# Requesting the later modulation weights from ScalarE's queue in a two-layer transformer step

## The chip, the cores and the metric

The kernel runs on one core of a Trainium2 chip, in one launch. The metric is the device time in microseconds. Three timed runs of the kernel before took 2960.68, 2961.05 and 2964.94 us. Beside them stands one profiled execution, from which all rows of the trace come.

A core has five engines that run side by side, each with its own stream of instructions in a fixed order: TensorE (PE, with its weight loads as PEld), VectorE (DVE), ScalarE (ACT), GpSimd (POOL) and SyncE (SP), which computes nothing and here requests transfers. A transfer between main memory and the core's own memory is requested by an instruction in the stream of one engine. If that instruction has to wait, everything behind it in the stream waits too. The data move later, on 16 DMA engines, and a semaphore tells when they have landed.

## The reference

One step of a diffusion backbone: two layers (DEPTH = 2) on 1024 sample tokens and 128 prompt tokens, width 1024, all in fp32. Cut to what matters here:

```python
def _modulation(cvec, w, b):
    m = (jax.nn.silu(cvec) @ w + b)[:, None, :]
    return jnp.split(m, 6, axis=-1)

def _layer(x, mod, lw, ctx):
    sh1, sc1, g1, sh2, sc2, g2 = mod
    h = _rms(x, n1) * (1 + sc1) + sh1
    u_conv, qa, ka, va, qn, kn, vn = jnp.split(h @ w_in, idx, axis=-1)
    ...
    x = x + g1 * (jnp.concatenate([a_out, b_out, c_out], axis=-1) @ w_out)
    h = _rms(x, n2) * (1 + sc2) + sh2
    x = x + g2 * (jnp.square(jax.nn.relu(h @ w1)) @ w2)
```

For each layer the modulation multiplies two conditioning vectors (one for the sample, one for the prompt) with a 1024 x 6144 matrix ada_w. The kernel cuts these 6144 columns into three groups of 2048: group 0 holds sh1 and sc1, which are needed at the start of the layer, group 1 holds g1 and sh2, group 2 sc2 and g2, which are needed after the attention.

## The kernel before

The program is written out in order by hand (the scheduler keeps the order of the source on every engine), with Python generators that are stepped in between one another. Waits and the choice of buffers are put in by the framework: a tile of the pool T gets one of 18 buffers of 128 x 512 fp32, and an instruction that writes a new tile waits until the last user of the buffer is done.

All transfers go through the helper `load` (L143), which takes an engine and uses SP where none is given. So SP requests everything: weights, stores of projections, loads for the attention, results.

`modulation(l, groups, first)` is a generator. Its `fetch` takes the next pair of group r and slab k of 128 rows of ada_w. In its later form (not `first`) it makes four T tiles `aw` of 128 x 512 and loads them (L203), 256 KB each. The generator fetches one slab ahead: a step runs the four matmuls of slab k (L224, shown as eight, since each fp32 matmul is two rows) into the bank `psmod`, and then fetches slab k + 1. After eight slabs a group is copied out and transposed. The first group of layer 0 goes another way (`first`, L198) and is not touched.

There are 40 fetches in three places. For layer 0, groups 1 and 2 (16 fetches) are stepped as `fill` from `project`; for layer 1, group 0 (8 fetches) is stepped from the last groups of layer 0's `mlp`, once for every two products, and groups 1 and 2 (16 fetches) again from `project`.

`project` multiplies the normed tokens with w_in, column block by column block: A0 to A5 and VN, each in five token groups of which the last is half as long. A token group on PE is `tok_group` (L548 to L550, rows `pst`). Behind it comes `post`: ACT squares (`sq`), DVE sums (`ss`), ACT takes logarithm and exponential (`y`), DVE refines and multiplies (`xn`), and POOL applies the gains and, in A0 and A1, the rotary embedding (L491 to L497, rows `o` and `t`). Between these stand steps of a convolution (rows `cacc`, `cp`). After the first, third and fifth group of a block `fill` is stepped once, and after every group `flush` requests the stores of `o` to `ddA` and `dvA` that are three groups old. After the second and fourth group's matmuls `pr.step` splits a piece of w_in (CAST `wh` on ACT, `wl` on DVE) and requests the next (`wr`). In A5 the first loads for the attention follow: keys `kd` and `cd`, values `v`, queries `qd`; the keys are transposed on PE (`pstr`, L791).

In `mlp` a product is 24 matmuls into a pair of banks (L1326), and `taken` moves it out, on ACT and DVE, to `ev`; `w1h` and `w1l` are the split weights of the products to come.

Of the kernel before, what the change touches and what calls it, by code (L numbers as in the profile page):

```python
# [45 lines left out]
def hybrid_step(ctx, tc, I, O, depth=DEPTH):  # L46
    nc = tc.nc
# [13 lines left out]
    def T(shape, dt=F32, n="t"):  # L61
        return pers.tile([128] + list(shape), dt, tag="T", bufs=N_T, name=nm(n))
# [24 lines left out]
    def P(n="ps"):  # L87
        return psum.tile([128, 512], F32, tag="p", bufs=8, name=nm(n))
# [9 lines left out]
    def tt(out, a, b, op, eng=None):  # L98
        (eng or nc.vector).tensor_tensor(out=out, in0=a, in1=b, op=op)  # L99

    def stt(out, a, s, b, op0, op1):
        nc.vector.scalar_tensor_tensor(out=out, in0=a, scalar=s, in1=b, op0=op0, op1=op1)  # L102
# [25 lines left out]
    def ada_b(l):  # L128
        return vecs[l][:, 0:48]

    def n1g(l):
        return vecs[l][:, 48:56]

    def n2g(l):
        return vecs[l][:, 56:64]
# [7 lines left out]
    def load(out, in_, eng=None):  # L143
        (eng or nc.sync).dma_start(out=out, in_=in_)
# [38 lines left out]
    def modulation(l, groups, first=False):  # L183

        todo = [(r, k) for r in groups for k in range(KT)]
        ready = []

        def fetch():
            if todo:
                r, k = todo.pop(0)  # L190
                if first:
                    if k % 2 == 0:
                        o = {0: 0, 2: 12, 4: 4, 6: 8}[k]
                        ready.extend([[HF[o + 2 * a + b][:, c:c + 512] for b in range(2) for c in (0, 512)] for a in range(2)])
                    o = {0: 0, 2: 12, 4: 4, 6: 8}[k - k % 2] + 2 * (k % 2)
                    for b in range(2):
                        c = r * 2048 + b * 1024
                        load(HF[o + b][:, 0:1024], I["ada_w"][l, k * 128:(k + 1) * 128, c:c + 1024])  # L198
                    return
                four = []  # L200
                for c in range(r * 2048, (r + 1) * 2048, 512):
                    aw = T([512], n="aw")
                    load(aw, I["ada_w"][l, k * 128:(k + 1) * 128, c:c + 512])  # L203
                    four.append(aw)
                ready.append(four)

        for _ in range(6 if first else 1):
            fetch()
        if first:
            ps = P("psmod")  # L210
            nc.vector.memset(ps, 0.0)
            yield
            fetch()
            fetch()
        yield
        for r in groups:
            if not first:
                ps = P("psmod")
                nc.vector.memset(ps, 0.0)
                yield  # L220
            for k in range(KT):
                aw = ready.pop(0)
                for j in range(4):
                    mm(ps[32 * j:32 * j + 2, :], silc[:, k, :], aw[j], start=(k == 0), stop=(k == KT - 1))  # L224
                if not first:
                    fetch()
                yield
            mt = T([512], n="mt")
            nc.vector.tensor_copy(mt, ps)
            yield  # L230
            pt = P("psmt")
            for b in range(4):
                nc.tensor.transpose(pt[:, b * 128:(b + 1) * 128], mt[:, b * 128:(b + 1) * 128], ident)
            ptv = pt.rearrange("p (b j x) -> p j b x", b=4, j=4, x=32)
            for s in range(2):
                tt(mod[l][:, s, r * 16:(r + 1) * 16].rearrange("p (j b) -> p j b", j=4), ptv[:, :, :, s],
                   ada_b(l)[:, r * 16:(r + 1) * 16].rearrange("p (j b) -> p j b", j=4), ALU.add)
            if r == 0:
                for s in range(2):
                    stt(A1[l][:, s, :], mod[l][:, s, 8:16], 1.0, n1g(l), ALU.add, ALU.mult)  # L240
            if r == 2:
                for s in range(2):
                    stt(A2[l][:, s, :], mod[l][:, s, 32:40], 1.0, n2g(l), ALU.add, ALU.mult)
            yield
# [1745 lines left out]
```

## Time and profile before

| | us |
|---|---|
| median of three timed runs | 2961.05 |
| lowest, highest | 2960.68, 2964.94 |
| the profiled execution | 2955.55 |
| its span, first to last instruction | 2953.8 |

The rows that the prediction quotes are of these kinds. The page gives busy times and the chain of work that ended last. The view of a tile gives, for all instructions that touch it, their number and their duration (least, median, most, in ns), the waits that it ended and, for transfers, the time from the request to the landing. A row of windows gives one stretch: its length, the busy time of PE, PEld, DVE, ACT and POOL with the number of instructions in brackets, PE's granted clock, the mean busy share of the DMA engines and GB/s. A row of the waits reads: who waited, for whom, us in total, how often, the longest. A row of the timeline reads: start, length, engine, line, operation, tiles written and read, shapes, how many instructions were merged, and in brackets the idle time of the engine before it and what ended it. SPq marks requests of SP; where several are merged into one row, its length contains the waits between them.

### The profile page before, as it was taken

The page shows a single profiled execution, that of the slowest core. Times are in us where ns is not written, and L with a number is a line of the kernel's source. Part 1 is how long each engine was busy: PE and PEld are TensorE (multiplying, and loading weights), DVE is VectorE, ACT ScalarE, POOL GpSimd, SP SyncE. Part 2 cuts the span into 40 slices and gives each one's busy share as a digit, 9 for nine tenths or more (in the row PEclk, how much of TensorE's full clock was granted, in tenths as well). Part 3 has the DMA queues.
Part 4 walks back from the last instruction along what each step waited for, and adds up shares of the span by engine and source line. Part 5 has one row for each costly group of instructions (what it writes and reads, how often), then busy time and mean ns, then how long its engine had stood idle before and what let it go on. Part 6 is the DMA issues. An engine that isn't in the chain of part 4 may idle for free.

```text
span 2953.8 us, 52917 instructions
## 1 busy us (share of the span) xinstructions
PE 2840.5 (96%) x20328; PEld 2520.6 (85%) x20328; DVE 2036.7 (69%) x4009; ACT 1413.2 (48%) x2924; POOL 658.6 (22%) x607
## 2 busy tenths in 40 slices
PE   6999999999999999999889999999999999999999
PEld 3879645899999989999878885458999999999999
DVE  6576778854867756668675757778467776585776
ACT  4335366762744443433452453668446444443343
POOL 3587346410000000000225772563100000000000
PEclk7999999999999999999989999999999999999999
DMA  7277202424466678542433781024345675665334
GB/s 289 81 217 195 83 22 56 103 83 134 159 204 220 193 241 302 164 149 91 139 123 105 191 219 50 17 69 99 97 122 196 199 221 176 217 226 183 114 105 161
DMA packets 434876, 444.05 MB, mean 150 GB/s; under 512 B 120512, under 2 KB 308672, under 8 KB 434624
## 3 DMA queue, kind: packets, MB, share of 16 engines
q1 hardware_dynamic: 434624, 440.67, 47.9%
q8 instruction: 160, 2.62, 0.4%
q14 instruction: 92, 0.75, 0.1%
HBM read 307.41 MB, written 133.17 MB: 149 GB/s over the span
## 4 chain that ended last, share of the span: by engine, by line
PE 82%; DVE 9%; ACT 3%; DMA 2%; issue 2%; POOL 2%; SPq 0%; DVEq 0%; POOLq 0%; ACTq 0%
PE ps L1326 24%; PE psb L1326 7%; PE psc L1326 6%; PE pso L1326 5%; PE psa L1326 5%; PE pst L548 4%; PE pst L549 3%; PE pst L550 3%; PE psd L1326 3%; PE psacc L1125 3%; PE pspv L992 2%; PE pspt L976 2%; PE psst L1139 2%; PE psmod L224 2%; PE psm L1051 2%
## 5 line engine op out<-in xcount | busy, mean ns | idle before, releaser
L1326 PE MATMUL ps<-ts,w2h 128*128 128x288 f32 x3072 | 535.5, 296 | 8.3 <-DVE ts L99 4.8
L1326 PEld LDWEIGHTS ps<-ts,w2h 128*128 128x128 f32 x3072 | 452.7, 189 | 9.3 <-DVE ts L99 5.3
L1326 PE MATMUL ps<-ts,w2l 128*128 128x288 f32 x1536 | 329.7, 296 | 0.0
L96 ACT CAST ts<-ti 128x576 fp32r<-128x576 f32 x256 | 172.1, 672 | 311.5 <-PE ps L1326 210.2
L548 PE MATMUL pst<-wh,HA 128*128 128x256 f32 x1040 | 295.4, 284 | 0.0
L549 PE MATMUL pst<-wl,HA 128*128 128x256 f32 x1040 | 291.8, 281 | 0.0
L550 PE MATMUL pst<-wh,HA 128*128 128x256 f32 x1040 | 291.6, 280 | 0.0
L93 ACT ACTIVATE ev<-ev 128x576 f32<-128x576 f32 x240 | 164.7, 686 | 259.8 <-DVE ev L99 256.0
L1326 PEld LDWEIGHTS ps<-ts,w2l 128*128 128x128 f32 x1536 | 247.8, 189 | 0.2
L99 DVE TENSOR_TENSOR ts<-ti,ts 128x576 fp32r<-128x576 f32 x256 | 195.1, 762 | 44.7 <-ACT ts L96 44.7
L102 DVE SCALAR_TENSOR_TENSOR X<-ps,mod,X 128x288 f32<-128x288 f32 x336 | 112.1, 409 | 164.8 <-PE ps L1326 164.8
L548 PEld LDWEIGHTS pst<-wh,HA 128*128 128x128 f32 x1040 | 195.7, 188 | 19.2 <-PE pst L550 5.2
L99 POOL TENSOR_TENSOR nacc<-nacc,nsq 128x512 f32<-128x512 f32 (+1 forms) x12 | 15.8, 1321 | 819.3 <-PE ps L1326 793.4
L550 PEld LDWEIGHTS pst<-wh,HA 128*128 128x128 f32 x1040 | 196.1, 189 | 0.0
L549 PEld LDWEIGHTS pst<-wl,HA 128*128 128x128 f32 x1040 | 195.9, 188 | 0.1
L1779 POOL COPY yu<-X 128x128 f32<-128x128 f32 x8 | 4.4, 559 | 835.3 <-DVE X L102 823.4
L1326 PE MATMUL pso<-HA,woh 128*128 128x288 f32 x1024 | 177.7, 295 | 0.0
L1053 DVE TENSOR_REDUCE mx<-psm 128x1 f32<-128x384 f32 x288 | 142.1, 547 | 30.7 <-PE psm L1051 30.6
L93 ACT ACTIVATE pt<-psst 128x512 f32<-128x512 f32 x216 | 118.2, 597 | 89.0 <-PE psst L1140 88.1
L99 POOL TENSOR_TENSOR R<-R,pt 128x1024 f32<-128x1024 f32 x60 | 149.4, 2489 | 26.0 <-ACT pt L93 24.0
L1326 PEld LDWEIGHTS pso<-HA,woh 128*128 128x128 f32 x1024 | 149.5, 188 | 0.0
L102 DVE SCALAR_TENSOR_TENSOR cacc<-cin,vecs,cacc 128x1167 f32<-128x1167 f32 x78 | 132.4, 1697 | 18.5 <-POOL cacc L577 17.3
(280 smaller groups left out, 7182.2 us busy)
## 6 DMA issues: line engine op xcount, KB each, us to landing
ti<-hd SPq DMA_DIRECT2D x128, 576.0 KB, 3.9
hd<-ev SPq DMA_DIRECT2D x224, 288.0 KB, 4.0
w1r<-in_mlp_w SPq DMA_DIRECT2D x176, 256.0 KB, 4.1
aw<-in_ada_w SPq DMA_DIRECT2D x160, 256.0 KB, 4.0
HF<-in_mlp_w SPq DMA_DIRECT2D x128, 256.0 KB, 5.0
ddA<-o SPq DMA_DIRECT2D x144, 128.0 KB, 3.5
wr<-in_w_in SPq DMA_DIRECT2D x28, 512.0 KB, 4.1
sd<-ev SPq DMA_DIRECT2D x24, 576.0 KB, 2.8
```

What stands on the lines that cost most here:

```text
L93: nc.scalar.activation(out=out, in_=in_, func=func, scale=scale, bias=bias, **k)
L96: nc.scalar.copy(out, in_)
L99: (eng or nc.vector).tensor_tensor(out=out, in0=a, in1=b, op=op)
L102: nc.vector.scalar_tensor_tensor(out=out, in0=a, scalar=s, in1=b, op0=op0, op1=op1)
L224: mm(ps[32 * j:32 * j + 2, :], silc[:, k, :], aw[j], start=(k == 0), stop=(k == KT - 1))
L548: mm(o, hi, wh, start=(k == 0), stop=False)
L549: mm(o, hi, wl, start=False, stop=False)
L550: mm(o, lo, wh, start=False, stop=(k == KT - 1))
L976: nc.tensor.transpose(ps[0:n, c], self.p[j][:, o:o + n], ident)
L1053: nc.vector.tensor_reduce(out=mx[j][:, qt, b:b + 1], in_=ps[:, 0:384], op=ALU.max, axis=AX.X)
L1125: mm(acc[64 * j:64 * j + 64, :], v, pt[:, j, :], start=(kt == 0), stop=(kt == 8))
L1326: mm(ps[h][:, 0:HH], x, y[:, h * HH:(h + 1) * HH], start=(start and z == 0), stop=(stop and z == 2), skip_group_check=True)
```

## The change

In `fetch`, the later form of the load names ScalarE, so that these 160 requests stand in ACT's stream of instructions, at the same place of the program, and not in SP's. The tiles, the slabs, the number of transfers and their sizes stay, and so does the first group of layer 0.

```diff
                 four = []
                 for c in range(r * 2048, (r + 1) * 2048, 512):
                     aw = T([512], n="aw")
-                    load(aw, I["ada_w"][l, k * 128:(k + 1) * 128, c:c + 512])
+                    load(aw, I["ada_w"][l, k * 128:(k + 1) * 128, c:c + 512], nc.scalar)
                     four.append(aw)
                 ready.append(four)
```

## The prediction

> **What bounds the kernel now.** I began with the profile page: the busy shares, then the chain that ended last.
>
> ```profile
> span 2953.8 us, 52917 instructions
> PE 2840.5 (96%) x20328; PEld 2520.6 (85%) x20328; DVE 2036.7 (69%) x4009; ACT 1413.2 (48%) x2924; POOL 658.6 (22%) x607
> PE 82%; DVE 9%; ACT 3%; DMA 2%; issue 2%; POOL 2%; SPq 0%; DVEq 0%; POOLq 0%; ACTq 0%
> ```
>
> TensorE (PE) is busy throughout and carries 82% of the chain. It executes in order, so I count each microsecond for which it stands before a modulation matmul in full. ScalarE (ACT) is about half idle, and SyncE's queue (SPq) is not on the chain. Second, the view of tile aw, and the busy times of the three stretches in which its transfers run.
>
> ```profile
> L144 SPq DMA_DIRECT2D aw<-in_ada_w x160: 327/384/2581, 107.4 to 1773.5; - x160
>   DMA aw<-in_ada_w: 33.6, 36
> DMA to landing us min/median/max: 2.7/4.0/6.7
> 100.00:335.00 235.00, 227.30 (x1794) 202.29 (x1793) 152.03 (x249) 90.06 (x199) 151.75 (x118) 1.00 0.63 175
> 1020.00:1105.00 85.00, 85.00 (x630) 75.86 (x629) 46.88 (x83) 37.14 (x72) 0.00 (x0) 1.00 0.67 225
> 1545.00:1800.00 255.00, 243.93 (x1849) 214.14 (x1849) 163.61 (x259) 100.33 (x216) 156.56 (x126) 0.98 0.59 164
> ```
>
> There are 160 requests in 40 fetches of four. Waits for aw add up to 33.6 us over PE's two rows, which overlap, so less than that is lost. In the window rows the fourth number in front of a bracket is ACT: 90 of 235, 37 of 85 and 100 of 255 us. ACT has room, so the question is where in its order the requests stand. One request takes a median 0.384 us on SP, and a transfer lands 4.0 us after it.
>
> **Part one: what is removed.** 160 requests times 0.384 us is 61 us of SP's issue time. It lies beside PE's work, since SPq has 0% of the chain, so I credit nothing for it directly. What could be worth more is that SP no longer stands at an aw request:
>
> ```profile
> 160.30 11.86 SPq L144 DMA_DIRECT2D aw<-in_ada_w  x4
> 1621.55 13.79 SPq L144 DMA_DIRECT2D aw<-in_ada_w  x4
> SPq L144 <- POOL t L495: 7.1, 1, 7.1
> 208.19 1.04 PE L224 MATMUL psmod<-aw,silc 128*2 128x512 f32 x8
> 183.17 1.65 PE L224 MATMUL psmod<-aw,silc 128*2 128x512 f32 x4 [0.59 <-DMA aw<-in_ada_w]
> 185.59 1.65 PE L224 MATMUL psmod<-aw,silc 128*2 128x512 f32 x4 [0.78 <-DMA aw<-in_ada_w]
> ```
>
> The two long fetches stand in SP until GpSimd (POOL) is done with rotary work whose T buffers aw reuses (the wait row is that of SP from 160 to 172 us; 1621 to 1635 has the same). Another queue does not give the buffer back sooner, so the weights come no earlier for the change. That a block of matmuls is starved now is seen in the last two rows: 183.17 to 187.24 for eight matmuls that take 1.04 at 208.19.
>
> **Part two: the wait moves into ACT.** The fetch of 160.30 belongs to the third token group of column block A1. On ACT it stands where that group's last y is done and a CAST of w_in begins now (165.09), and it is over when SP was done with it, at 172.16. Behind it are that CAST and the fourth group's sq:
>
> ```profile
> 165.09 1.04 ACT L96 CAST wh<-wr 128x1024 fp32r<-128x1024 f32 x1
> 169.91 0.60 ACT L93 ACTIVATE sq<-pst 128x512 f32<-128x512 f32 x1 [3.78 <-issue]
> 168.49 1.29 DVE L99 TENSOR_TENSOR wl<-wr,wh 128x1024 fp32r<-128x1024 f32 x1
> 170.55 0.69 DVE L420 TENSOR_REDUCE ss<-sq 128x8 f32<-128x512 f32 x1 [0.77 <-ACT sq L93]
> 179.58 0.42 DVE L99 TENSOR_TENSOR xn<-pst,y 128x256 f32<-128x256 f32 x1 [0.31 <-POOL t L495]
> 178.42 3.47 SPq L144 DMA_DIRECT2D aw<-in_ada_w  x4
> SPq L144 <- DVE xn L99: 1.6, 1, 1.6
> ```
>
> CAST 172.16 to 173.2, then sq to 173.8; on DVE, wl behind the CAST to 174.5 and ss to 175.2, where it ended at 171.24: 3.9 late. DVE works in order, so the fifth group's xn is late by 3.9 less the 0.31 it waited for POOL: 3.6. The next fetch waits for that very xn (last two rows), and its matmuls are the starved ones of 183.17. So PE loses **3.6 us**, and as much in the second layer (1621.55): 7.2. Bounds: nothing, if its slot is another one; 7.1 each (165.09 to 172.16) if the whole block arrives on PE.
>
> **Part three: requests that ACT reaches late.** The fetch after a block's fifth group is used one group later, only 6.8 us after the previous use (208.19, above, to 215.01). SP ran ahead there; ACT reaches it only after that group's activations:
>
> ```profile
> 202.66 1.86 SPq L144 DMA_DIRECT2D aw<-in_ada_w  x4
> 211.19 0.25 ACT L96 COPY o<-pst 128x128 f32<-128x128 f32 x1
> 215.01 1.04 PE L224 MATMUL psmod<-aw,silc 128*2 128x512 f32 x8
> 266.84 0.21 ACT L93 ACTIVATE y<-y 128x4 f32<-128x4 f32 x1
> 270.00 1.04 PE L224 MATMUL psmod<-aw,silc 128*2 128x512 f32 x8
> ```
>
> No request of ACT's is in this trace. I take SP's 0.384 and a little between (1.86 for four is 0.46 each), the nearest row; the bounds are nothing and SP's longest, 2.58. Then the fourth request leaves 1.4 us after the first and lands 4.0 later: 5.4 after ACT gets there. In block A2, 211.4 plus 5.4 is 216.8; the last matmuls end near 217.1 instead of 216.05: 1.1. In A4, 267.05 plus 5.4 is 272.5, end 272.8 instead of 271.04: 1.8. In A5, where other matmuls stand between, I set nothing, and where two groups lie between fetch and use the 5.4 fits. Two layers: **5.8 us**. Requests that cost nothing take 1.4 from each, which leaves 0.4 in A4, 0.8 in all; requests of 2.58 add three times 2.15, 6.5, to each of the four places, some 32 in all. In the MLP's stretch ACT gets there earlier in one place and later in others:
>
> ```profile
> 1048.80 0.71 ACT L93 ACTIVATE ev<-psa 128x288 f32<-128x288 f32 x2 [0.41 <-PE psa L1326]
> 1051.16 1.88 SPq L144 DMA_DIRECT2D aw<-in_ada_w  x4
> 1056.33 2.12 PE L224 MATMUL psmod<-aw,silc 128*2 128x512 f32 x8
> ```
>
> ACT could ask at 1049.5 instead of 1051.16, which takes the 1.1 us from the block at 1056.33; the other fetches come later but lie two products apart, so I set this stretch at nothing (1 us either way).
>
> **Part four: SP waits for ACT.** SP's requests stand behind the landing of earlier, unrelated ones:
>
> ```profile
> 282.32 1.96 SPq L144 DMA_DIRECT2D aw<-in_ada_w  x4
> 284.32 2.09 SPq L144 DMA_DIRECT2D ddA<-o  x4
> 286.63 0.36 SPq L144 DMA_DIRECT2D dvA<-o  x1
> 287.38 2.71 SPq L144 DMA_DIRECT2D ddA<-o  x4
> SPq L144 <- DMA aw<-in_ada_w: 0.8, 3, 0.3
> 266.37 1.97 SPq L144 DMA_DIRECT2D aw<-in_ada_w  x4
> 269.68 2.09 SPq L144 DMA_DIRECT2D ddA<-o  x4
> 271.81 1.07 SPq L144 DMA_DIRECT2D kd<-ddA  x1
> 271.68 0.36 ACT L96 COPY o<-pst 128x256 f32<-128x256 f32 x1
> 277.37 0.63 PE L791 MATMUL pstr<-ident,kd 128*128 128x128 f32 x4 [0.44 <-ACT sq L93]
> ```
>
> The stores of 287.38 use nothing of aw, yet wait three times for aw to land (the wait row is that of 287.3 to 289.6). They stand eight places behind: I read it as a rotation of eight completion counters, each of which must be full before it is used again. If both queues share the rotation, SP stops eight places behind a fetch until ACT has issued it. The costliest place is the first key load kd: eighth behind the fetch of 266.37 (four aw, four ddA), and PE takes it at once, after a wait of 0.44. ACT reaches that fetch at 272.04 (end of the o copy), its first transfer lands at 276.0, and kd leaves then instead of at 271.81: **4.2 us** late, 8.4 in both layers. Bounds: 0 with separate counters; some 55 us if each of the 32 fetches in the two projection stretches delayed PE by ACT's four requests (four times 0.43).
>
> **Sum**: 7.2 + 5.8 + 8.4 = 21.4 us onto the profiled execution's own 2955.55 us (its span and 1.75 around it): 2976.95. The median of the timed runs, 2961.05, lies 5.5 higher; the forecast on it is **2982.5 us**.
>
> One rule of the Trainium skill speaks on the change. DMA: Bandwidth & Descriptors, in "Issuing engines are not separate DMA queues", says that transfers asked for by several engines run on the same 16 DMA engines and that spreading the requests saves the sequencer's issue time alone; this trace has one queue only and cannot show it. By that rule alone nothing is won here and nothing lost, which is the second rival. The same page's "Queues, rings and completion order" says that each DMA engine takes turns between SP's and ACT's rows; no run here shows that either, and if it brought every landing from the median 4.0 to the fastest 2.7, the six places of parts three and four would lose up to 1.3 us less each, and the sum would be about 14.
>
> **Rivals.**
> - *Faster: the freed SP returns buffers.* While SP stands at 160.30 and 1621.55, stores of o wait behind it, and o lies in the same T buffers that aw, xn and sq need. If these come free earlier, the starved blocks shrink: the one of 183.17 holds 3.0 us, and all of them at most about half of the doubled 33.6, 17. That would give 2944, half of it 2952.5. It decides where a slot waits for a store. Against it: in both long fetches the longest wait ended with POOL's t (7.1 us), which no queue changes.
> - *No change, 2961.* ACT is idle more than half of each stretch, and in most fetches SP's request left long before its use. Against it: 6.8 us between uses leave no room for 5.4 plus 2 to 4 us of activations.
> - *Separate counters.* No 8.4: 2974.
> - *A cascade.* ACT late, aw late, stores late, buffers late, ACT later. With the 55 us: 3016.
>
> **Chances and range.** The sum as worked out 0.30, separate counters 0.22, cascade 0.15, no change 0.18, faster 0.15. What this kernel's measurement can tell from no change is about 0.2%, 6 us, so: slower 0.67, same 0.18, faster 0.15. The likeliest case alone runs from 2970 to 2995; eight times in ten the time should lie between 2950 (half of the faster rival) and 3008 (short of the full cascade).
>
> **What would show it.** Part two: an ACT stretch of about 7 us in which aw requests stand before a CAST, and a wait before psmod in A2 of some 7 us in place of 4. Part three: waits for aw before the blocks that now run in 1.04. Part four: kd issued at aw's landing, and a wait of about 4 us before pstr. If waits for aw at PE shrink below 33.6 us, or the requests of ACT take well under 0.38 us, the forecast is too high; if POOL's or DVE's waits for stores of o grow, it is too low.

## The result, and the profile after

The median of four timed runs after the change is 3004.36 us (3001.85 to 3005.47), beside 2960.86 for the kernel before on the same chip: 43.5 us slower, a ratio of 1.0149 with a 95% interval of 1.013 to 1.0167. The forecast was 2982.5, 21.4 us up. The sign and the range held; the size was half.

The page of the profiled execution after the change (span; busy times; the chain that ended last, by engine):

```profile
span 3003.1 us, 52815 instructions
PE 2867.0 (95%) x20328; PEld 2527.2 (84%) x20328; DVE 2027.3 (68%) x4009; ACT 1414.8 (47%) x2924; POOL 649.1 (22%) x607
PE 75%; DVE 9%; ACT 4%; POOL 4%; DMA 4%; issue 3%; SPq 1%; ACTq 0%; POOLq 0%; DVEq 0%
```

The busy times of DVE, ACT and POOL are those of before within 10 us: none of them got more work. PE's rose by 26.5 us with the same 20328 instructions. Of this, 21.3 lie in the psmod matmuls on aw (56.8 to 78.1 us), which overlap less when their weights come one by one and some of which took 1.06 us instead of 0.59. PE's share of the chain fell from 82 to 75%, and DMA's and POOL's rose from 2 to 4%.

PE's granted clock was 0.86 from 150 to 200 us and 0.93 from 1600 to 1700, where it was 1.00 before: around the starved sets of fetches 1 and 4, in both layers, it was halved for 6.8 us each. From the end of such a set to the end of the next, PE fell behind by 0.55 to 0.70 us, 2.5 in all; inside a set the clock's part can't be told from the wait's. The view of tile aw says for whom PE stands:

```profile
L144 ACTq DMA_DIRECT2D aw<-in_ada_w x160: 334/388/945, 121.9 to 1831.0; - x160
...
  DMA aw<-in_ada_w: 91.1, 56
...
  PEld psmod L224: 60.5, 40
  PE psmod L224: 30.6, 16
...
DMA to landing us min/median/max: 2.7/3.9/8.4
```

A request costs ACT what it cost SP (0.388 us against 0.384), and a transfer still lands 3.9 us after it (4.0). But the waits for aw went from 33.6 us in 36 places to 91.1 in 56 (over PE's two rows, which overlap). In the median the transfers are as fast as before, though the slowest took 8.4 us and not 6.7; most of the loss comes of their being asked for later.

Where the time went can be read from the ends of the 40 sets of psmod matmuls, which stand at the same place of PE's order in both kernels. For fetch 7, the fifth group of A2, the set ends at 215.01 + 1.04 = 216.05 before and at 226.70 after: 10.65 us behind. The growth of this lag, added up over both layers, in us (two profiled executions differ by up to some 3 us in a stage where the kernels are the same):

| where the weights are used | forecast | after |
|---|---|---|
| A0 and A1 (fetches 0 to 4) | 7.2 | 9.9 |
| A2 to A4, with the first key load (5 to 11) | 5.8 + 8.4 | 17.6 |
| A5 and VN (12 to 15) | 0 | 16.5 |
| MLP | 0 | 3.8 |
| elsewhere | 0 | 1.6 |
| span | 21.4 | 49.3 |

Layer 0's fetch 0 holds 1.7 of the 9.9. It was 0.6 to 2.6 us behind before in the kernels below that ask for it on SP, too, so this part can't be put down to the change. (Layer 1's fetch 0, 1.6, is counted under elsewhere.) The spans differ by more than the medians, since the profiled execution of before lies 5.3 us under its median.

The fifth group of A2 shows the kind of loss. From the timelines of ACT, SP and PE, after the change:

```profile
217.56 0.33 ACTq L144 DMA_DIRECT2D aw<-in_ada_w  x1
217.93 4.90 ACTq L144 DMA_DIRECT2D aw<-in_ada_w  x3
222.88 0.60 ACT L93 ACTIVATE sq<-pst 128x512 f32<-128x512 f32 x1 [3.80 <-DMA ddA<-o]
...
220.10 1.91 SPq L144 DMA_DIRECT2D ddA<-o  x4
...
221.57 1.70 PE L224 MATMUL psmod<-aw,silc 128*2 128x512 f32 x6
225.68 1.02 PE L224 MATMUL psmod<-aw,silc 128*2 128x512 f32 x2 [2.41 <-DMA aw<-in_ada_w]
```

ACT begins at 217.56, and the row of three contains a wait: the fourth request left at 222.50, 4.9 us after the first, where the forecast had 1.4. It stood until the first of the stores that SP asked for at 220.10 had landed, at 222.42. It uses nothing of that store. The built program names the semaphore that both share (here the two instructions, with what each adds to or waits for):

```
ACT  aw323_2136 <- in_ada_w      waits DMAHW4_49, DMAHW2_49    adds to DMAHW4_49
SP   ddA2_0_120 <- o305_2053     waits DMAHW4_49, Pool_49      adds to DMAHW4_49
```

All transfers of SP and ACT take eight such counters in strict turn, 1500 of 1500 in the built program's list, and each waits until the one before it on its counter is complete. The turn was fixed when the program was built; there these stores stand ahead of the requests, although the source has them behind. So a request of ACT's can wait for a store that SP has not even asked for yet, and SP asks for it only when POOL has made its o. Behind the request, the next group's sq waited 3.80 us. The waits of ACT's own instructions for transfers of others are a new kind of row. Before there was one:

```profile
ACT sq L93 <- DMA ddA<-o: 1.7, 1, 1.7
```

After:

```profile
ACT sq L93 <- DMA ddA<-o: 16.5, 4, 4.5
ACT k L96 <- DMA aw<-in_ada_w: 11.8, 2, 6.7
ACT wh L96 <- DMA ddA<-o: 10.2, 2, 5.2
ACT k L96 <- DMA ddA<-o: 8.1, 2, 4.1
ACT sq L93 <- DMA aw<-in_ada_w: 8.0, 3, 2.9
ACT wh L96 <- DMA aw<-in_ada_w: 4.7, 1, 4.7
...
SPq L144 <- DMA aw<-in_ada_w: 38.4, 27, 3.1
```

sq, k and wh read neither ddA nor aw: what waits is a request in front of them. Summed request by request from the trace's semaphore events (no view has this as one row), ACT's 160 requests stood 69.5 us, 56.6 of it for stores to ddA. Whether these are waits of the counters or of T buffers whose last tile is still being stored can be read as well, from the semaphore of each wait and the address of each tile in the built program. Of 62.8 us that requests stood for landings, 62.1 ended with the transfer ahead on their own counter, whose tile lies in another buffer, and 0.7 with a store out of the buffer that aw takes over. The last row is the other direction: SP, too, waits for ACT's transfers, 2.7 us before.

In A5 and VN four sets a layer lose 16.5 us. A group of A5 has five stores (as one of A2 has), and ACT also splits the attention's keys (k) there; which weighs more no run separates:

```profile
308.95 1.06 ACT L96 CAST k<-pstr 128x512 fp32r<-128x512 f32 x2 [6.74 <-DMA aw<-in_ada_w]
...
314.62 0.33 ACTq L144 DMA_DIRECT2D aw<-in_ada_w  x1
314.99 5.07 ACTq L144 DMA_DIRECT2D aw<-in_ada_w  x3
320.10 1.15 ACT L96 CAST k<-ones 1x1152 fp32r<-1x1152 f32 x1 [4.09 <-DMA ddA<-o]
...
316.52 1.91 SPq L144 DMA_DIRECT2D ddA<-o  x4
...
321.61 1.02 PE L224 MATMUL psmod<-aw,silc 128*2 128x512 f32 x2 [1.95 <-DMA aw<-in_ada_w]
324.16 1.85 PE L224 MATMUL psmod<-aw,silc 128*2 128x512 f32 x2 [1.53 <-DMA aw<-in_ada_w]
```

Four requests from 314.62 to 320.06, where the same fetch took SP 1.85 before (290.98 to 292.83). PE stands twice, and ACT's casts of k stand 6.74 and 4.09 us.

### The profile page after: what moved, and what is told of

It reads as the page before. It is cut to its first block, busy times and chain, and to the rows that moved or that the text cites. A ratio compares the mean times of both kernels' runs of the same rounds, so it can differ in the third digit from the quotient of the medians.

```text
span 3003.1 us, 52815 instructions
## 1 busy us (share of the span) xinstructions
PE 2867.0 (95%) x20328; PEld 2527.2 (84%) x20328; DVE 2027.3 (68%) x4009; ACT 1414.8 (47%) x2924; POOL 649.1 (22%) x607
## 4 chain that ended last, share of the span: by engine, by line
PE 75%; DVE 9%; ACT 4%; POOL 4%; DMA 4%; issue 3%; SPq 1%; ACTq 0%; POOLq 0%; DVEq 0%
PE ps L1326 23%; PE psb L1326 8%; PE psc L1326 6%; PE pso L1326 5%; PE psa L1326 5%; PE psd L1326 3%; PE psacc L1125 3%; PE pspv L992 2%; PE pspt L976 2%; PE pst L548 2%; PE psst L1139 2%; PE pst L549 2%; PE pst L550 2%; PE psm L1051 2%; DMA aw<-in_ada_w 1%
## 5 line engine op out<-in xcount | busy, mean ns | idle before, releaser
L99 DVE TENSOR_TENSOR w1l<-w1r,w1h 128x512 fp32r<-128x512 f32 x128 | 88.0, 689 | 86.4 <-ACT w1h L96 86.4
```

## The experiments

My theory after the two traces: ACT's requests are late in its order, and they wait for landings of stores that have nothing to do with them (C, the counters). The rivals: lateness alone (L), the T buffers of stored o (S), or a cost that every request of ACT's has (N). The first runs set P, the place of a fetch, whatever makes it costly there, against N.

**The change by parts.** Which fetches are on ACT is chosen in `fetch`; with q counting the 16 fetches of a projection:

```diff
+                on_act = groups != [0] and (r - 1) * KT + k in (1, 4, 7, 10, 13)
...
-                    load(aw, ..., nc.scalar)
+                    load(aw, ..., nc.scalar if on_act else None)
```

e1_fifth has the fetches at fifth groups on ACT, e2_rest the projection's others (`not in`), e3_mlp the eight of the MLP (`groups == [0]`).

> Only the fetches at a block's fifth token group (10 of the 40, 40 requests) are asked for by ACT. Theory P (place: such a fetch is used one group later, and on ACT it starts late and waits for landings): by the growth of the starved blocks in the trace of after (2.6, 3.1, 4.1, 2.5 and 6.3 us in layer 0, as much in layer 1) this run carries 30 to 37 of the 43 us: about 2991 to 2998. Rival N (number: every request of ACT's costs alike, by holding ACT and through late stores): 10 of 40 fetches are a quarter, 11 us: 2972.

Measured: 2991.76, ratio 1.0092 (1.0075 to 1.0109), 30.3 us over the 2961.51 of before in that call.

> The other 22 fetches of the two projection stretches are asked for by ACT, those at the fifth groups and the MLP's by SP. Theory P: 3 to 10 us over before, 2964 to 2971, since these fetches are used two groups or more after they are asked for. Rival N: 22 of 40, 24 us: 2985. It holds the long fetch of A1's third group; if what is lost there (3.6 us a layer by the prediction) comes of its holding ACT, 7 us: 2968.

Measured: 2968.17, 1.0023 (1.0011 to 1.0035), 6.7 us.

> Only the eight fetches in the MLP (layer 1's first group) are asked for by ACT. If the parts add up, what the first two runs leave of the 43 us: 43.5 less 30.3 less 6.7 is 6.5, so 2965 to 2969; the trace of after has this stretch 3.8 us later than before, which would be 2965. By the prediction (nothing, 1 us either way): 2960 to 2962. Rival: the parts do not add up, and the MLP's share is nothing alone.

Measured: 2966.76, 1.0023 (1.0009 to 1.0037), 6.8 us over 2960.00; in its profile the MLP's own lag grew by 3.3.

N falls: 40 requests of 160 carry most. The three parts add up to 43.8 us against 43.5, but that is partly chance. By place they don't add: in A5 and VN e1_fifth lost 3.6 us and e2_rest 0.4, and all together 16.5; in A0 and A1 e1_fifth lost 19.4, and all together 9.9. Of the 19.4, 12.5 arose at fetch 1 of the two layers, where the fourth request stood 4.7 and 4.4 us for a store out of the very buffer that it takes over: in e1_fifth rival S is real, while after has 0.7 us of it. And e2_rest's loss is not where any theory had it. Requests, key load and transpose in A5 of e2_rest, from its timelines:

```profile
272.94 2.02 ACTq L144 DMA_DIRECT2D aw<-in_ada_w  x4
...
276.29 0.63 SPq L144 DMA_DIRECT2D kd<-ddA  x1
...
282.22 0.80 PE L792 MATMUL pstr<-ident,kd 128*128 128x128 f32 x4 [4.37 <-DMA kd<-ddA]
```

This is part four of the prediction as it stands there: the fetch of A5's first group is on ACT, SP stops eight places behind it, kd leaves when the first aw has landed, and PE waits. In after the same key load costs nothing:

```profile
286.60 0.63 SPq L144 DMA_DIRECT2D kd<-ddA  x1
...
292.84 0.60 PE L791 MATMUL pstr<-ident,kd 128*128 128x128 f32 x4
```

No wait stands before it: PE is late itself, through the starved fetch 10 just ahead, and 6.2 us lie between request and use.

**Stores on another queue.** `flush` asks POOL, with aw on ACT (pst_act) and on SP (pst_sp).

```diff
-            load(out, in_)
+            load(out, in_, nc.gpsimd)
```

> As after, and the delayed stores of y, k and v (ddA, dvA and the outputs) are asked for by POOL instead of SP. To be compared with the next run alone, which has the same stores on POOL and aw on SP. Theory C (ACT's requests wait because a completion counter of theirs was last used by a store of SP's that has not landed): if POOL's stores use other counters, ACT's waits for ddA (56.6 us in after) fall below 10 us and the difference to the next run to 10 to 20 us. Rival S (aw waits for the T buffer of an o whose store has not landed): the wait stays, whatever queue stores, above 35 us, and so does a difference of 35 to 50. Rival L (ACT gets to the fetch late, waits or not): the waits may go, but the difference stays at 35 or more.

> As before, with the delayed stores on POOL: the control of the run above. No theory says much of it alone; POOL is 22% busy and a store's request takes its time there, so 2955 to 2985.

Measured: 3053.04 and 3051.25. The pair differs by 1.8 us, but the move costs 90 by itself, outside what I had expected of the control:

```profile
L144 POOL DMA_DIRECT2D ddA<-o x216: 706/750/924, 144.2 to 1868.1; - x108
```

216 requests of 0.75 us stand in POOL's order among its rotary work, and everything behind it is late in both. In pst_act requests still waited 38.8 us for ddA by the same sum as above; POOL's stores use counters of their own, so these are waits for buffers (S), in a kernel whose stores are late. The pair tells nothing between C and L. It doesn't carry S over to after either, whose own trace has 0.7 us of it.

**Two moves that take lateness and fresh stores away.** early_act and early_sp put the fill step ahead of the group's post, so that ACT meets the requests before sq, y and o. odd_act and odd_sp let stores leave only at the second and fourth group, where nothing is fetched.

```diff
 # early
+                if g % 2 == 0:
+                    next(fill, None)
                 two = post(L, c, t, nt, ps)
...
-                if g % 2 == 0:
-                    next(fill, None)
 # odd
-        while stores and (every or stores[0][0] <= 0):
+        while go and stores and (every or stores[0][0] <= 0):
...
-                flush()
+                flush(go=g % 2 == 1)
```

> As after, but in the projection each fill step (matmuls and next fetch) stands before the group's post instead of behind it, so ACT meets the requests before that group's sq, y and o, some 2 to 4 us earlier; the order on PE is the same. To be compared with early_sp. Theory P (place in ACT's order): the fifth group's weights land in time, the difference to early_sp falls from 43 to 5 to 15 us. Theory C (waits for the landing of SP's stores, which stand in front of the requests in the rotation of completion counters): the stores are as near as before and now hold that group's sq as well: the difference stays at 30 or more.

> As before, with the same move of the fill steps: the control of early_act. SP already ran ahead, so little changes: 2950 to 2970; buffers are taken in another order (aw ahead of the group's o and xn), which may cost where T is short.

Measured: 3001.36 and 2962.73, apart by 38.6 us. L alone falls: earlier requests wait longer. The waits of early_act:

```profile
ACT sq L93 <- DMA ddA<-o: 40.5, 9, 9.2
```

> As after, but in the projection the delayed stores leave SP only at token groups without a fill step (the second and fourth of a block), so that at a fetch the last stores are a group old. To be compared with odd_sp. Theory C (ACT's requests wait for the landing of stores that SP has just asked for): these have landed, ACT's waits for ddA fall from 56.6 us to under 15, and the difference of the pair from 43 to 10 to 20 us. Rival L (ACT gets to the fetch too late, whatever it waits for): the waits may fall but the difference stays at 35 to 45.

> As before, with the stores at the second and fourth group alone: the control of odd_act. Some y, k and v stay in T for a group or two longer: 2958 to 2975.

Measured: 2996.06 and 2965.34, apart by 30.7. The summed waits for ddA fell from 56.6 to 20.1, not under 15, and the loss by less than C said: it is neither alone. So both at once, odd_early_act, with odd_early_sp as its control.

> Both moves at once, aw on ACT: fill steps ahead of the group's post, stores only at the second and fourth group. If C and L each hold a part of the loss, this one is free of both and lies 3 to 15 us over before: 2964 to 2976. If C alone matters, it equals odd_act. If neither, it stays at 2995 to 3005.

> Both moves with aw on SP, the control: odd_sp and early_sp lie 4 and 3 us over before, so 2960 to 2970. Then odd_early_act costs 14 to 24 us more than its control, by the trace of odd_early_act in A5 and VN, where a fetch still meets stores of k and v.

Measured: 2984.24, which no answer named, and 2960.98 (1.0004, 0.9994 to 1.0014: the moves themselves cost nothing that can be told). 23.3 us are left of 43.5; the two ran on different chips, and by their ratios to before it is 22. By place, as in the table above, the kernel on ACT less its control on SP:

| | A0, A1 | A2 to A4 | A5, VN | MLP |
|---|---|---|---|---|
| after (less before) | 9.9 | 17.6 | 16.5 | 3.8 |
| early | 4.8 | 14.7 | 16.7 | 4.2 |
| odd | -5.0 | 11.0 | 18.9 | 1.9 |
| both | -1.8 | 1.5 | 17.7 | 3.7 |

The -5.0 is the control's: the profiled execution of odd_sp is itself 11.2 us behind before in A0 and A1. Either move leaves most of the loss in A2 to A4, both leave 1.5 of 17.6 (5.3 and 5.5 in mid_moved and no_tail below). A5 and VN are as bad as ever. In odd_early_act, the timeline of ACT there:

```profile
297.80 5.11 ACTq L144 DMA_DIRECT2D aw<-in_ada_w  x4
303.03 0.28 ACT L93 ACTIVATE sq<-pst 128x128 f32<-128x128 f32 x1 [5.09 <-DMA dvA<-o]
...
307.56 3.86 ACTq L144 DMA_DIRECT2D aw<-in_ada_w  x2
311.46 0.59 ACT L96 COPY o<-pst 128x512 f32<-128x512 f32 x1 [3.50 <-DMA out_new_na_k<-o]
```

The stores held back leave SP in one row of about twenty, 0.5 us apart (290.67 to 303.42), so the next fetch meets them all the same.

**Which blocks.** mid_plain has only the six fetches asked for in A2 to A4 on ACT, in the order of before; mid_moved the same six with both moves. tail_only has those asked for in A5 and VN on ACT; no_tail is odd_early_act with fetches 11 to 15 back on SP (five a layer by the edit, k < 11; its expectation counts four).

```diff
+                on_act = groups != [0] and (r - 1) * KT + k in range(5, 11)
 # tail_only
+                on_act = groups != [0] and (r - 1) * KT + k >= 11
 # no_tail
+                on_act = groups == [0] or (r - 1) * KT + k < 11
```

> Only the fetches asked for in blocks A2 to A4 (six a layer) are on ACT, in the order of before. The blocks of A2 to A4 fell behind by 9.6 us in layer 0 and 8.1 in layer 1 in the trace of after: both theories, C and L, say 14 to 20 us over before, 2975 to 2981. Rival: what was lost there came of earlier trouble in A0 and A1, and then it is 5 us or less.

Measured: 2981.79, 1.0078 (1.0065 to 1.0091), 23.0 over before's 2958.78, a little over both theories' 14 to 20; 19.9 of its profile's lag arose in A2 to A4.

> The same six fetches a layer on ACT, with fill steps ahead of the post and stores at the second and fourth group alone. If late requests and waits for just issued stores are all that ACT's queue costs, the difference to odd_early_sp is 0 to 3 us here, against 14 to 20 without the moves. If there is a third cost (the requests' own time on ACT, the turn of the transfers), it stays above 8.

Measured: 2966.66, 5.7 over odd_early_sp. Between the two answers, but 17 of 23 us went. What is left is lateness by itself. ACT in A4's fifth group of mid_moved:

```profile
269.53 0.30 ACT L93 ACTIVATE y<-ss,eps 128x8 f32<-128x8 f32 x1 [3.14 <-DVE ss L421]
...
270.16 0.34 ACTq L144 DMA_DIRECT2D aw<-in_ada_w  x1
270.62 1.33 ACTq L144 DMA_DIRECT2D aw<-in_ada_w  x3
```

No wait stands at these requests (the summed waits for ddA are 0), but y ahead of them waited 3.14 us for DVE, and the set that uses the weights ended 3.4 us later than it should; 2.2 in layer 1.

> Only the fetches asked for in A5 and VN (five a layer) are on ACT, in the order of before. If they cost by themselves what A5 and VN lost in after (16.5 us in both layers): 2972 to 2979. Rival: the loss there needs ACT to be late already from the blocks ahead; then 3 to 8 us: 2962 to 2968.

Measured: 2978.34, 1.0058 (1.0042 to 1.0075), 18.8 over before's 2959.57. The number fits the first answer, its reason doesn't: A5 and VN hold 7.1 us of it, and 8.1 stand before them, at the two key loads (4.4 and 3.7). Layer 0:

```profile
278.78 0.62 SPq L144 DMA_DIRECT2D kd<-ddA  x1
...
283.65 0.63 PE L792 MATMUL pstr<-ident,kd 128*128 128x128 f32 x4 [3.32 <-DMA kd<-ddA]
```

> As odd_early_act, with the last four fetches of each layer (asked for in A5 and VN) back on SP; the other 28 of the projection stretches' 32 less 4, and the MLP's eight, on ACT. If the 18.6 us of A5 and VN hang on these requests, it lies 3 to 9 us over odd_early_sp's 2961: 2964 to 2970. If ACT's other requests hold that loss, it stays at 2978 to 2986.

Measured: 2967.95, 1.0026 (1.0016 to 1.0036), 7.0 over odd_early_sp, on another chip. With five fetches a layer back on SP the lag in A5 and VN, against before, is 0.4 us where it was 18.6. Fetch 11, which stands ahead of the first key load, is among the five. The rest is the MLP's 3.6 and what mid_moved has.

**Another queue with counters of its own.** early_pool is early_act with `nc.gpsimd` in place of `nc.scalar`.

> As early_act, but POOL's queue asks for aw; the requests of POOL's queue have completion counters of their own. Read by stages. In blocks A2 to VN of layer 0 (fetches 5 to 15) early_act falls 17.3 us further behind before. Theory C: with counters of its own and early in its engine's order a request goes at once, though it takes about 0.75 us on POOL: at most 5 us there. Rival Q (a queue of an engine that computes is late in itself): 12 us or more there. In A0 and A1 POOL's rotary work stands ahead of the requests, so the first fetches may lose more than on ACT; over all 2970 to 3010.

Measured: 3021.34, 1.0202 (1.0178 to 1.0226), above the 2970 to 3010 expected. From fetch 5 to 15 of layer 0 it fell 14.9 us behind, which is Q's answer. In its tile view a request takes POOL 0.54 us:

```profile
L144 POOL DMA_DIRECT2D aw<-in_ada_w x160: 538/538/708, 114.9 to 1840.0; - x160
```

Counters of one's own don't help where the engine gets to its requests late; both layers' A0 and A1 lose 36.0 us here, behind the rotary work.

**Better on SP?** skip_sp leaves the fill steps out of A0 and A1, part_sp has the early step in A0 and A1's first four groups.

```diff
 # skip_sp
-                if g % 2 == 0:
+                if g % 2 == 0 and c not in ("A0", "A1"):
 # part_sp
+                ahead = c == "A0" or c == "A1" and g < 4
+                if g % 2 == 0 and ahead:
+                    next(fill, None)
                 two = post(L, c, t, nt, ps)
...
-                if g % 2 == 0:
+                if g % 2 == 0 and not ahead:
```

> As before, but no fill step in blocks A0 and A1, where the projection shares T with the rotary work; the steps left out there run later, in the attention. In the trace of before the starved blocks there (fetches 1, 3, 4 and the same in layer 1) take 4.35, 4.16, 4.07, 4.69, 4.59 and 4.03 us instead of 1.04 each: 19.6 us over. Theory: the later steps find their weights in time, 2941 to 2950. Rival: PE would wait for the rotary work there in any case, or the later steps cost the same: 2958 to 2964.

> aw on SP, fill steps ahead of the post only in A0 and in A1's first four groups. early_sp was 4.3 us ahead of before after the third fetch of layer 0 and 6.7 us in layer 1, and lost it at A1's fifth group, where the step now stands as in before. If the gain keeps: 2949 to 2955. Rival: what was gained is a debt that the next block pays, because PE waits for the rotary work and the buffers it frees: 2958 to 2963.

Measured: 2965.65 (1.0013, 1.0004 to 1.0023) and 2971.06 (1.0045, 1.0029 to 1.0061). Both rivals were right in kind and too mild. part_sp was 4.5 us ahead at fetch 3 and lost 10.9 at fetch 4: what is gained at one starved set of A0 or A1 is lost at the next. That it is owed to the rotary work is argued, not shown, and no trace here shows where skip_sp lost its 5.7 us. No version here beats the kernel before.

## Why the prediction was right in sign and wrong in size

- **Part one holds.** SP's freed 61 us brought nothing.
- **Part two: the place was right, the sum not.** ACT stands in the long fetch of A1 and the next set is starved:

```profile
169.79 5.80 ACTq L144 DMA_DIRECT2D aw<-in_ada_w  x4
175.63 1.06 ACT L96 CAST wh<-wr 128x1024 fp32r<-128x1024 f32 x1 [5.64 <-POOL o L497]
...
189.23 3.92 PE L224 MATMUL psmod<-aw,silc 128*2 128x512 f32 x8 [3.88 <-DMA aw<-in_ada_w]
```

Fetch 4 lost 3.1 us in either layer, for 3.6 forecast. But the set before it, fetch 3, came 2.1 and 2.5 us nearer, so the pair nets 1.7 and not 7.2. And in e2_rest, which has the long fetch on ACT and fetch 4 on SP, fetch 4 lost only 0.9 and 0.4: holding ACT is not enough, the next fetch has to be on ACT too. In after, fetch 4's first request also stood 1.8 us, in either layer, for a store that only shares its counter. A0 and A1 as a whole still lost 9.9, most of it at fetches 1 (2.6 twice), where requests stand 2.4 us for such stores. That this is near the 7.2 is luck.
- **Part three failed in its term "the fourth request leaves 1.4 us after the first", and in "In A5, where other matmuls stand between, I set nothing".** The 1.4 was 4.9 in A2 and 5.1 in A5; in A4 it held (1.5 and 1.3). A2's fifth groups lost 4.1 and 5.1 us where 1.1 was set, A4's 2.5 and 2.7 where 1.8 was: 14.3 for the 5.8. A5 and VN lost 16.5 where nothing was set, and that is most of what the forecast lacks. The mechanism of the term, a request that ACT reaches late, is real (mid_moved still has it, 3.4 and 2.2), but it was priced without the waits in front of the request. no_tail and mid_moved show that the losses hang on these requests; odd_early_act shows that in A2 to A4 the larger part needs lateness and fresh stores together.
- **Part four: mechanism right, and covered.** Shared counters are real, SP stood 38.4 us for ACT's aw, and by itself it costs what was set: 4.37 us of wait in e2_rest, 3.32 in tail_only, for 4.2. In after PE is late at that place already, and nothing is added (the set behind the key load came 0.6 and 0.8 us nearer). So 17.6 beside the 14.2 forecast for A2 to A4 is luck: 8.4 of the 14.2 didn't come, and part three's places lost more than twice their share. What I didn't see is the other direction of the same turn of eight: I asked what stands behind ACT's requests on SP and not what stands ahead of them. SP can afford to wait, since it runs ahead; ACT has the next group's work behind it.
- **The MLP, set at nothing,** lost 3.8, and 6.8 by the median of e3_mlp. In after the sets of fetches 19 and 23 fell behind there, by 2.4 and 2.3 us. Fetch 19 before and after, each time beside SP's next requests for weights:

```profile
1053.61 2.09 SPq L144 DMA_DIRECT2D aw<-in_ada_w  x4
1055.79 3.08 SPq L144 DMA_DIRECT2D w1r<-in_mlp_w  x4
...
1082.88 2.04 SPq L144 DMA_DIRECT2D w1r<-in_mlp_w  x4
1083.38 1.85 ACTq L144 DMA_DIRECT2D aw<-in_ada_w  x4
```

No counter holds these requests. ACT asks 6.0 us ahead of the use, where SP asked 11.3 ahead, and beside SP's four w1r instead of in front of them; the last of the four landed 6.9 us after its request (5.8 before), and for fetch 23 it was 8.4 (3.8 before). With the median of 4.0 both would have come in time. That the w1r beside them delay them is read from the order; no run shows it.
- **The rivals.** The cascade (3016) was nearest, and the one whose words fit: ACT late, aw late, ACT later. That SP's freed time returns buffers is not shown: fetch 3 came nearer, but in early_sp, where SP asks, it did so too (2.7 and 3.1 us). The shorter landings that would have made the sum about 14 did not come (a median of 3.9 us against 4.0). No change was also what follows from the rule of the Trainium skill in DMA: Bandwidth & Descriptors, "Issuing engines are not separate DMA queues", taken alone. The trace agrees with it in so far as the median landing stayed and SP's freed 61 us brought nothing; what was lost lies in the requests' waits, 69.5 us on ACT.

That the shared counters hold ACT's requests is read from the built program and the trace, request by request (62.1 of 62.8 us). No run took the sharing away and left all else; the pair with POOL's stores was meant to and didn't. So what PE would lose without the sharing stays open, in A0 and A1 above all, where requests also wait for POOL.

## What to carry to other kernels

A transfer's request is an instruction that can wait, and on a queue with little slack behind it the wait costs, not the 0.39 us of the request. Before moving requests to an engine that computes, list what each of them waits for in the built program, the completion counters that it shares with other queues' transfers included, in both directions, and look at what stands behind it on that engine. The half idle engine was no better a place here than the one that does nothing but wait.

## What was not expected of the hardware and the program

- A request of one queue waited for a transfer that another queue had not yet asked for (ACT from 218.91 to 222.50 for a store of 220.10), since the turn of the counters is fixed when the program is built.
- The same stall changes its price with its surroundings: the late key load costs PE a wait of 4.37 us in e2_rest and nothing in after, and the fifth groups' fetches alone lost more in A0 and A1 (19.4) than the whole change (9.9).
- On POOL, requests took 0.54 us for aw (0.38 on SP, 0.39 on ACT) and 0.75 for ddA (0.50 on SP), in the median.
- A median hides what a request's neighbours do: in the MLP's two late sets aw took 6.9 and 8.4 us to land, while the median over all 160 went from 4.0 to 3.9.
